# A weights-ring buffer for the window branch's key/value tiles, sets of four for two kinds of scores, and modulation products that wait for their last load

## The chip, the cores and the metric

One NeuronCore of one Trainium2 chip runs the whole kernel. The metric is the device time of one execution in microseconds (us); lower is better. The change is judged by the median of timed runs of the kernel before and after.

## The reference

One decoder layer for a prompt of 512 tokens and for 8 sample sequences of one token each, in float32. The layer's input is modulated by a vector that comes from a product with `w_ada`; one projection feeds a state-space branch (S5) and an attention branch with compressed, selected and window keys; then an output projection and an MLP follow.

```python
def hybrid_layer(x, c, ssm_s0, attend, lp):
    mod = jnp.dot(jax.nn.silu(c), lp['w_ada']) + lp['b_ada']        # 1024 -> 6144, for 1 + 8 rows
    sh1, sc1, gt1, sh2, sc2, gt2 = jnp.split(mod, 6, axis=-1)
    h = modulate(x, lp['norm_attn'], sh1, sc1)                      # rmsnorm(x) * (1 + sc1) + sh1
    proj = jnp.dot(h, lp['w_in'])
    u, q, k_c, v_c, k_s, v_s, k_w, v_w, g = jnp.split(proj, offsets, axis=-1)
    ...
    o_ssm, s_last = ssm_mixer(u, ssm_s0, lp)
    o_attn, win_state = attend(q, gates, kv_cmp, kv_slc, kv_win)
    mix = jnp.concatenate([rmsnorm(o_ssm, ...), rmsnorm(o_attn, ...)], axis=-1)
    x = x + gt1[:, None, :] * jnp.dot(mix, lp['w_out'])
    h2 = modulate(x, lp['norm_mlp'], sh2, sc2)
    x = x + gt2[:, None, :] * jnp.dot(jnp.square(jax.nn.relu(jnp.dot(h2, lp['w_up']))), lp['w_down'])
    return x, kv_cmp, kv_slc, win_state, s_last

def nsa_block(q, gates, ..., k_cmp, v_cmp, k_blk, v_blk, k_band, v_band, ...):
    p_cmp = masked_softmax(jnp.einsum('bgrqd,bngd->bgrqn', q, k_cmp), ...)
    ...                                          # the 16 best blocks are chosen from p_cmp
    p_slc = masked_softmax(jnp.einsum('bgrqd,bgqkjd->bgrqkj', q, k_sel), ...)
    p_win = masked_softmax(jnp.einsum('bgrqd,bkgd->bgrqk', q, k_band), ...)
```

The new keys and values (`kv_cmp`, `kv_slc`, `kv_win`) are outputs too.

## The kernel before, in words

**Who sets the order.** The kernel is written as straight code in Tile, and the framework is built with a scheduler that places every instruction on its engine's queue by a time that it models for it. Each queue then runs strictly in that order. So a dependence that the code adds changes the order of many instructions, not only of the one that waits. Loads go out on SyncE's queue (SP), most stores of the projections on ScalarE's (ACT), gathers on GpSimd's (POOL).

**Modulation (`ada`, lines 334 to 356).** The 6144 outputs are computed in 12 chunks of 512 columns, `ada0` to `ada11`. A chunk loads 1024x512 weights, in four loads of 512 KB or two of 1 MB (line 344, tile `wada`), and issues 8 products (line 348, tile `pada`): the stationary operand `cT[:, k]` has 32 columns, and product `k` writes rows `k % 4 * 32` of the result, so products 0 to 3 use four different groups of 32 columns of TensorE's array, and 4 to 7 add to them. ACT copies the result out (line 350), four transposes turn it (line 353, `padt`), and VectorE (DVE) sums it into `mod` (line 355). Chunks 0 to 3 are shift and scale of the first modulation; `hf`, `hH` and `hL` (lines 213 to 215), the modulated input as a high and a low part, need them, and the projection `pj` (line 619) needs `hH` and `hL`. The products `ph` (line 401), which compress the cached keys and values, and their transposes `pxc` (line 382) fill the first stage beside it.

**Key/value projections (`kv_proj`, from line 635).** Called for the compressed (0), selected (1) and window (2) branch. For each of four blocks of 128 tokens, ACT copies the result `pkv` into a tile `kvt` (line 672 or 688), sends it out by DMA (lines 673, 691, 692), and two transposes `pkt` (line 695) read it. `kvt` comes from a pool with two buffers. The large weights (`wkv`, `wq`, `wglu`, the halves of `wada`, `wo`, `wup`, `wdn`) come from a ring of three buffers, `rawt(name)`, each 128x2048 floats; a new tile waits until its buffer's last reader is done. `wq` (line 917) holds the queries' weights, which ACT and DVE split into `wH` and `wL` (lines 66, 67) for the query projection, again `pj`. `yc` (line 903) are small loads of the state-space branch's result, `rwin` (line 1165) the window rows of the sample sequences.

**Scores.** `compressed_scores` (from line 1170) computes `psc`: two sets of four products 128x32 by 128x512, one per head, each into its own 32 rows; the head's queries are ready after DVE's subtraction into `QS` (line 929). `sample_keys` (from line 1028) is called four times: for each set of four sequences, 16 transposes `pkT` (line 1038) and four copies `ktS` (lines 1041 and 1043, ACT for even, DVE for odd) give the keys, and four products `pS` (line 1047) the scores, again each into its own 32 rows. Six such sets exist. Between them lies the prompt's attention (`pst`, lines 1232 to 1234; `ptp`, line 1261; `po`, line 1268).

**State-space steps.** `u` is stored to scratch memory (`uscr`, lines 632 and 633) and loaded in another layout (`U<-uscr`, line 735), and `pvs` (line 805) reads it.

The dense end (`pwo`, `pup`, `pdn`, line 1427) takes the rest of the time.

Of the kernel before, what the change touches and what calls it, by code (L numbers as in the profile page):

```python
# [17 lines left out]
P = 128  # L18
# [19 lines left out]
def body(tc, i, o, dbg=None):  # L38
# [22 lines left out]
        return bank["tile"].tile([P, 512], F32, tag=tag, name=name, bufs=bank["tags"][tag])  # L61

    banks("pA", pj=2, ss=2, tr=2, ad=1, po=1)

    def split(h, l, src):
        nc.scalar.copy(h, src)  # L66
# [266 lines left out]
    def ada(s, tag, parts=2):  # L333

        ps = pst(tag, "pada")
        kp = KT // parts
        rs = []
        for n in range(parts):
            if parts == 2:
                r = rawt("wada")  # L340
            else:
                r = wp.tile([P, 1120], F32, tag=("wH", "wL")[n % 2], name="wada", bufs=2)[:, 0:1024]
            r = r.rearrange("p (k c) -> p k c", k=kp)
            nc.sync.dma_start(r, i["w_ada"][0, n * kp * P : (n + 1) * kp * P, s * 512 : (s + 1) * 512].rearrange("(k p) c -> p k c", p=P))
            rs.append(r)

        for k in range(KT):
            nc.tensor.matmul(ps[k % 4 * 32 : k % 4 * 32 + 32], cT[:, k], rs[k // kp][:, k % kp], start=(k < 4), stop=(k >= 4))
        mrow = wp.tile([P, 520], F32, tag="mrow", name="mrow")[:, 0:512]
        nc.scalar.copy(mrow, ps)  # L350
        pt = pst(tag, "padt")
        for m in range(4):
            nc.tensor.transpose(pt[:, m * P : (m + 1) * P], mrow[:, m * P : (m + 1) * P], ident)
        ms = mod[:, 4 * s : 4 * s + 4]
        nc.vector.tensor_reduce(ms, pt.rearrange("p (m q c) -> p m c q", m=4, q=4)[:, :, 0:9], AX.X, ALU.add)
        nc.vector.tensor_tensor(ms, ms, v_ada[:, 4 * s : 4 * s + 4].unsqueeze(2).to_broadcast([P, 4, 9]), ALU.add)
# [276 lines left out]
            nc.sync.dma_start(uscr[q * P : (q + 1) * P, T:NT], uT[q][:, T:NT])  # L633

    onames = ("cmp", "slc", "win")

    def kv_proj(c):
        c0 = 1024 + 256 * c
# [7 lines left out]
        for kk in range(2):  # L646
            kr = slice(4 * kk, 4 * kk + 4)
            h, l = whl(4, nw)
            split(h[:, :, 0:256], l[:, :, 0:256], r[:, kr])
            if c == 2:  # L650
                split(h[:, :, 256:280], l[:, :, 256:280], rg[:, kr])
            ws.append((h, l))
        for t in range(5):
            tok = slice(t * P, t * P + (P if t < 4 else NB))
            mp = P if t < 4 else NB
# [10 lines left out]
                else:  # L666
                    nc.scalar.dma_start(o["new_win_sample"][:, T - 1], kvs[:, 512:768])
            else:
                kvt = p1.tile([P, 256], F32, tag="kvt", name="kvt", bufs=2)
                out = o["new_%s_prompt" % onames[c]][tok]  # L670
                if c == 0:
                    nc.scalar.copy(kvt, ps[:, 0:256])
# [242 lines left out]
    for s in range(2):  # L915
        r = rawt("wq").rearrange("p (k c) -> p k c", k=KT)
        nc.sync.dma_start(r, i["w_in"][0, :, 512 + s * 256 : 512 + (s + 1) * 256].rearrange("(k p) c -> p k c", p=P))
        for m in range(2):
            wh, wl = wsplit(r[:, :, m * P : (m + 1) * P])
            h0 = 2 * (2 * s + m)  # L920
            for hf, ps in proj_half(wh, wl):
                ql = wp.tile([P, 520], F32, tag="mrow", name="ql")[0:64].rearrange("p (a b) -> p a b", a=2)
                w = min(HB, T - hf * HB)
                for hh in range(2):
                    pq_ = ps[hh * 64 : hh * 64 + 64]
                    qc = (h0 + hh, slice(hf * HB, hf * HB + w))
                    nc.scalar.activation(ql[:, hh], pq_, AF.Copy, scale=HD**-0.5)
                    nc.scalar.activation(QS[0:64, *qc], pq_[:, 0:w], AF.Copy, scale=HD**-0.5)
                    nc.vector.tensor_tensor(QS[64:128, *qc], ql[:, hh, 0:w], QS[0:64, *qc], ALU.subtract)
            nc.gpsimd.tensor_copy(qs[:, h0 : h0 + 2], ql[:, :, HB - NB : HB])  # L930
        state_space_outputs((2 + s,))
    dump("gates", gates)
# [96 lines left out]
    def sample_keys(br, grp, tiles, nj, gate):  # L1029
# [3 lines left out]
        for h in range(nj // 4):  # L1033
            kts = []
            for b4 in range(4):
                px = pst(("ad", "ss")[b4 % 2], "pkT")
                for j4 in range(4):
                    nc.tensor.transpose(px[:, j4 * P : (j4 + 1) * P], tiles[b4][:, 4 * h + j4, 0:P], ident)  # L1038
                kt = sb.tile([P, 512], F32, tag="ktS", name="ktS", bufs=4)
                if b4 % 2:  # L1040
                    nc.vector.tensor_copy(kt, px)
                else:
                    nc.scalar.copy(kt, px)
                kts.append(kt)
            S = pst("ss", "pS")
            for b4 in range(4):
                nc.tensor.matmul(S[b4 * 32 : b4 * 32 + 32], q4[:, 4 * grp + b4], kts[b4], start=True, stop=True)  # L1047
            if br == 0:
                nc.vector.tensor_tensor(t[:, h * 512 : (h + 1) * 512].rearrange("p (j k c) -> p j k c", j=4, c=8),
                                        S.rearrange("p (j k c) -> p j k c", j=4, c=8),  # L1050
# [119 lines left out]
    def compressed_scores():  # L1170
        for g in range(2):
            ps = pst("ss", "psc")
            for hh in range(4):
                nc.tensor.matmul(ps[hh * 32 : hh * 32 + 32], Kcp[:, g], QS[:, 4 * g + hh].bitcast(F32), start=True, stop=True)  # L1174
            nc.scalar.copy(etc[:, g], ps)

    held = {}
# [72 lines left out]
    def values(br, h0, pes, po):  # L1250

        kb = 2 * br + h0 // 4
        for part in (((0, 0),), ((1, 0), (3, 3 * P)), ((2, 0),)):
# [12 lines left out]
            for kt, c0 in part:  # L1266
                for hh, PT in enumerate(PTs):
                    mm = nc.tensor.matmul(po[hh * 64 : hh * 64 + 64, kt * P : T], Vx[:, kt, kb], PT[:, c0 : c0 + T - kt * P],  # L1268
                                          start=(br == 0 and kt == 0), stop=False)
                    if hh == 0:  # L1270

                        tc.add_manual_dep(mm.ins, turned_.ins.name, mybir.DependencyInfo(mybir.DependencyClass.Sync, mybir.DependencyReason.DATA))

    glu_w = []
    mixs = {}
# [354 lines left out]
```

## Time and profile before

| | |
|---|---|
| median of 3 runs | 900.21 us (898.96 to 900.66) |
| profiled execution, device time | 896.71 us |
| its span in the trace | 895.0 us |
| TensorE busy (PE) | 845.8 us, 94% |
| VectorE (DVE) | 519.8 us, 58% |
| ScalarE (ACT) | 389.9 us, 44% |
| dense end, 520 to 895 us | PE busy 366.98 of 375 us |

The span is the time between the first and the last instruction of the trace; the device time has 1.71 us around it. The profiled execution is 3.5 us below the median of the timed runs. A float32 product stands in the trace as two records, so "x4" of such a product is two matmuls. In a timeline row, the number behind the start is the length of a group of like instructions in a row; "[1.67 <-DMA ...]" is the time that the engine stood idle before it and what ended that.

### The profile page before, as it was taken

Reading aid. Unit: us, or ns where it says so; the run is one execution under the profiler, and the core shown is the slowest. Engines: PE = TensorE matmul, PEld = TensorE weight load, DVE = VectorE, ACT = ScalarE, POOL = GpSimd, SP = SyncE. Lnnn points to the kernel's source line nnn. Section 1 sums busy time; section 2 is a strip of 40 time slices with the busy share of each in tenths; the row PEclk is TensorE's granted clock in tenths of the full one; section 3 lists DMA queues with packets and bytes.
Section 4 is the critical chain, followed back from the end, with each engine's and each line's share of the span. In section 5 each row is a group of like instructions: output and inputs, shape, how many; then the busy total and the mean of one; then the engine's idle time right before and its main releaser. Section 6 shows DMA issues by size and latency. Waiting matters only on the chain.

```text
span 895.0 us, 16400 instructions
## 1 busy us (share of the span) xinstructions
PE 845.8 (94%) x6527; PEld 751.8 (84%) x6527; DVE 519.8 (58%) x1365; ACT 389.9 (44%) x883; POOL 64.0 (7%) x147
## 2 busy tenths in 40 slices
PE   2799998999998999998989999999999999999996
PEld 1557997888987766756679989999999999999996
DVE  5876666785766466668667874442333444434533
ACT  1555317453435466556655554442111344433322
POOL 6001201000152100000000000000000000000000
PEclk9999998999999999999989999999999999999998
DMA  8957577473773441203266553333333333232302
GB/s 290 319 195 247 181 157 193 138 247 116 203 244 92 165 166 64 77 2 142 73 210 198 180 190 94 94 96 94 95 95 95 94 95 92 82 86 75 92 1 96
DMA packets 111836, 122.36 MB, mean 137 GB/s; under 512 B 24500, under 2 KB 91880, under 8 KB 109584
## 3 DMA queue, kind: packets, MB, share of 16 engines
q1 hardware_dynamic: 101968, 88.66, 32.8%
q0 software_dynamic: 5488, 29.99, 9.6%
q10 hardware_dynamic: 4304, 2.66, 1.1%
q8 instruction: 51, 0.84, 0.4%
q14 instruction: 25, 0.20, 0.1%
HBM read 112.47 MB, written 13.03 MB: 140 GB/s over the span
## 4 chain that ended last, share of the span: by engine, by line
PE 66%; DVE 2%; ACT 1%; issue 0%; ACTq 0%; DVEq 0%
PE pup L1427 21%; PE pdn L1427 21%; PE pwo L1427 5%; PE pj L619 3%; PE po L1268 2%; PE ptp L1261 2%; PE pg L1289 2%; PE pS L1047 2%; PE pst L1232 1%; PE pkT L1038 1%; PE pst L1233 1%; PE psc L1174 1%; PE pstat L879 1%; PE poS L1136 0%; PE po L1349 0%; PE pst L1234 0%
## 5 line engine op out<-in xcount | busy, mean ns | idle before, releaser
L1427 PE MATMUL pdn<-hidH,wL 128*128 128x256 f32 (+1 forms) x480 | 136.0, 283 | 0.0
L1427 PE MATMUL pdn<-hidL,wH 128*128 128x256 f32 (+1 forms) x480 | 135.8, 283 | 0.0
L1427 PE MATMUL pup<-h2L,wH 128*128 128x256 f32 (+1 forms) x480 | 135.5, 283 | 0.0
L1427 PE MATMUL pdn<-hidH,wH 128*128 128x256 f32 (+1 forms) x480 | 135.3, 282 | 0.0
L1427 PE MATMUL pup<-h2H,wL 128*128 128x256 f32 (+1 forms) x480 | 135.0, 282 | 0.0
L1427 PE MATMUL pup<-h2H,wH 128*128 128x256 f32 (+1 forms) x480 | 134.5, 283 | 0.0
L1427 PEld LDWEIGHTS pup<-h2L,wH 128*128 128x128 f32 x480 | 90.4, 188 | 0.8 <-DVE rs L105 0.8
L1427 PEld LDWEIGHTS pup<-h2H,wH 128*128 128x128 f32 x480 | 89.8, 188 | 0.8 <-ACT h2H L66 0.8
L1427 PEld LDWEIGHTS pdn<-hidH,wL 128*128 128x128 f32 x480 | 90.4, 188 | 0.0
L1427 PEld LDWEIGHTS pdn<-hidL,wH 128*128 128x128 f32 x480 | 90.2, 188 | 0.1
L1427 PEld LDWEIGHTS pup<-h2H,wL 128*128 128x128 f32 x480 | 90.3, 188 | 0.0
L1427 PEld LDWEIGHTS pdn<-hidH,wH 128*128 128x128 f32 x480 | 90.3, 188 | 0.0
L66 ACT CAST wH<-wdn 128x1024 fp32r<-128x1024 f32 x30 | 31.5, 1049 | 114.2 <-PE pdn L1427 104.3
L67 DVE TENSOR_TENSOR wL<-wup,wH 128x1024 fp32r<-128x1024 f32 x30 | 36.7, 1225 | 57.9 <-ACT wH L66 57.9
L67 DVE TENSOR_TENSOR wL<-wdn,wH 128x1024 fp32r<-128x1024 f32 x30 | 36.8, 1225 | 54.3 <-ACT wH L66 54.3
L401 PE MATMUL ph<-xc,w 128*128 128x256 f32 (+2 forms) x320 | 62.9, 346 | 0.7 <-DVE xc L391 0.7
L401 PEld LDWEIGHTS ph<-xc,w 128*128 128x128 f32 x320 | 50.8, 194 | 11.0 <-issue 5.4
L66 ACT CAST wH<-wup 128x1024 fp32r<-128x1024 f32 x30 | 31.5, 1050 | 47.3 <-PE pup L1427 37.5
L1507 ACT ACTIVATE rl<-pup 128x256 f32<-128x256 f32 (+1 forms) x64 | 24.5, 385 | 45.5 <-PE pup L1427 45.4
L389 ACT COPY xc<-pxc 64x256 f32<-64x256 f32 x96 | 32.1, 366 | 22.5 <-DVE xc L391 18.8
L1508 DVE TENSOR_TENSOR rl<-rl 128x256 f32<-128x256 f32 (+1 forms) x64 | 27.2, 426 | 22.9 <-ACT rl L1507 22.9
L1436 DVE SCALAR_TENSOR_TENSOR xT<-pdn,mod,xT 128x256 f32<-128x256 f32 x32 | 15.2, 478 | 41.7 <-PE pdn L1427 41.6
(569 smaller groups left out, 2038.8 us busy)
## 6 DMA issues: line engine op xcount, KB each, us to landing
wada<-w_ada SPq DMA_DIRECT2D x20, 1024.0 KB, 5.1
wup<-w_up SPq DMA_DIRECT2D x16, 1024.0 KB, 5.4
wdn<-w_down SPq DMA_DIRECT2D x16, 1024.0 KB, 5.7
wo<-w_out SPq DMA_DIRECT2D x8, 1024.0 KB, 5.5
wada<-w_ada SPq DMA_DIRECT2D x8, 512.0 KB, 16.0
rwin<-state_win SPq DMA_DIRECT2D x4, 1024.0 KB
new_win_sample<-state_win POOLq DMA_DIRECT2D x2, 2044.0 KB, 8.6
wkv<-w_in SPq DMA_DIRECT2D x3, 1024.0 KB, 8.1
```

The lines of the kernel that those rows point to most:

```text
L66: nc.scalar.copy(h, src)
L67: nc.vector.tensor_tensor(l, src, h, ALU.subtract)
L389: nc.scalar.copy(dst[:, :, :, hf], srcv[:, :, :, hf])
L401: nc.tensor.matmul(phv[:, lo:hi, 0:w], w1[n][:, r_], xc[n][:, lo:hi, r_ % 8, off : off + w], start=(r_ == 0), stop=(r_ == 15))
L619: nc.tensor.matmul(ps[:, 0:HB], w[:, k], x[:, k, hc], start=(k == 0 and n == 0), stop=(k == KT - 1 and n == 2))
L1047: nc.tensor.matmul(S[b4 * 32 : b4 * 32 + 32], q4[:, 4 * grp + b4], kts[b4], start=True, stop=True)
L1261: nc.tensor.transpose(pt_[:, c : c + P], at(qt, kt * P, P), ident)
L1268: mm = nc.tensor.matmul(po[hh * 64 : hh * 64 + 64, kt * P : T], Vx[:, kt, kb], PT[:, c0 : c0 + T - kt * P], start=(br == 0 and kt == 0), s ...
L1289: nc.tensor.matmul(ps[:, 0:HB], r[:, k, c], zf[k][:, hc], start=(k == 0), stop=(k == 3))
L1427: nc.tensor.matmul(ps[:, 0 : b - a], w, x[:, a:b], start=first and n == 0, stop=last and n == 2)
L1507: nc.scalar.activation(rl, ps[:, 0 : b - a], AF.Relu)
L1508: nc.vector.tensor_tensor(rl, rl, rl, ALU.mult)
```

## The change

Four edits and a helper. `not_before(mm, last)` adds a dependence: matmul `mm` is not started before `last` is done. The existing dependence in the prompt's value products now goes through the helper and stays as it was.

- In `ada`, the first of the 8 products waits for the chunk's last load, where before each product waited for its own part of the weights.
- In `kv_proj(2)`, the four tiles `kvt` are four quarters of one buffer of the weights' ring, where before they came from the pool of two.
- In `sample_keys`, the first of the four products `pS` waits for the copies of the third and the fourth key tile.
- In `compressed_scores`, the first of the four products `psc` waits for the last head's subtraction into `QS`.

```diff
+    def not_before(mm, last):
+
+        tc.add_manual_dep(mm.ins, last.ins.name, mybir.DependencyInfo(mybir.DependencyClass.Sync, mybir.DependencyReason.DATA))
...
-            nc.sync.dma_start(r, i["w_ada"][0, n * kp * P : (n + 1) * kp * P, s * 512 : (s + 1) * 512].rearrange("(k p) c -> p k c", p=P))
+            landed = nc.sync.dma_start(r, i["w_ada"][0, n * kp * P : (n + 1) * kp * P, s * 512 : (s + 1) * 512].rearrange("(k p) c -> p k c", p=P))
             rs.append(r)
 
         for k in range(KT):
-            nc.tensor.matmul(ps[k % 4 * 32 : k % 4 * 32 + 32], cT[:, k], rs[k // kp][:, k % kp], start=(k < 4), stop=(k >= 4))
+            mm = nc.tensor.matmul(ps[k % 4 * 32 : k % 4 * 32 + 32], cT[:, k], rs[k // kp][:, k % kp], start=(k < 4), stop=(k >= 4))
+            if k == 0:
+                not_before(mm, landed)
...
+    qlast = {}
...
+        kvr = rawt("kvt") if c == 2 else None
...
-                kvt = p1.tile([P, 256], F32, tag="kvt", name="kvt", bufs=2)
+                kvt = kvr[:, t * 256 : (t + 1) * 256] if c == 2 else p1.tile([P, 256], F32, tag="kvt", name="kvt", bufs=2)
...
-                    nc.vector.tensor_tensor(QS[64:128, *qc], ql[:, hh, 0:w], QS[0:64, *qc], ALU.subtract)
+                    qlast[h0 + hh] = nc.vector.tensor_tensor(QS[64:128, *qc], ql[:, hh, 0:w], QS[0:64, *qc], ALU.subtract)
...
-                if b4 % 2:
-                    nc.vector.tensor_copy(kt, px)
-                else:
-                    nc.scalar.copy(kt, px)
-                kts.append(kt)
+                kts.append((kt, (nc.scalar.copy, nc.vector.tensor_copy)[b4 % 2](kt, px)))
             S = pst("ss", "pS")
             for b4 in range(4):
-                nc.tensor.matmul(S[b4 * 32 : b4 * 32 + 32], q4[:, 4 * grp + b4], kts[b4], start=True, stop=True)
+                mm = nc.tensor.matmul(S[b4 * 32 : b4 * 32 + 32], q4[:, 4 * grp + b4], kts[b4][0], start=True, stop=True)
+                if b4 == 0:
+
+                    not_before(mm, kts[2][1])
+                    not_before(mm, kts[3][1])
...
-                nc.tensor.matmul(ps[hh * 32 : hh * 32 + 32], Kcp[:, g], QS[:, 4 * g + hh].bitcast(F32), start=True, stop=True)
+                mm = nc.tensor.matmul(ps[hh * 32 : hh * 32 + 32], Kcp[:, g], QS[:, 4 * g + hh].bitcast(F32), start=True, stop=True)
+                if hh == 0:
+                    not_before(mm, qlast[4 * g + 3])
```

How the scheduler's order moves is shown at three places. In these rows, "x8" counts instructions, and the changed kernel's line numbers are a few higher (348 becomes 352, 353 becomes 359, 401 becomes 407).

First, TensorE in the first stage, where chunk 0's products stand among the compression's products. Before (its first two products stand a few rows earlier):

```order
L348 MATMUL pada<-wada,cT 32x512 x2
L401 MATMUL ph<-xc,w_160 128x128 x3
L348 MATMUL pada<-wada,cT 32x512 x2
L401 MATMUL ph<-xc,w_160 128x128 x6
L449 MATMUL pss<-ones,xsq 8x1 x8
L401 MATMUL ph<-xc,w_160 128x128 x3
L401 MATMUL ph<-xc,w_161 128x130 x3
L348 MATMUL pada<-wada,cT 32x512 x2
L401 MATMUL ph<-xc,w_161 128x130 x13
```

Changed:

```order
L407 MATMUL ph<-xc,w_160 128x130 x4
L449 MATMUL pxs<-ident,xsr 128x64
L407 MATMUL ph<-xc,w_160 128x128 x16
L407 MATMUL ph<-xc,w_161 128x130
L455 MATMUL pss<-ones,xsq 8x1 x8
L407 MATMUL ph<-xc,w_161 128x130 x14
L352 MATMUL pada<-wada,cT 32x512 x8
L407 MATMUL ph<-xc,w_161 128x130
```

The four runs of two are one run of eight, behind 35 products `ph`. Of all chunks: before, the runs are 2+2+2+2 (chunk 0), 1+2+1+4 (chunk 1), 4+4 (chunks 2 to 6), 5+3 (7), 2+6 (8) and 8 (9 to 11); changed, 5+3 (chunk 4), 1+4+3 (chunk 8) and 8 for each other. `psc` goes from six runs (2, 2, 1, 1, 1, 1) to two of four, and `pS` from 13 runs to six of four.

Second, TensorE ahead of the first projection `pj`, where chunk 3, the last that the modulated input needs, is turned (`padt`). `px` are the transposes of the input itself. Before:

```order
L348 MATMUL pada<-wada,cT 32x512 x4
L592 MATMUL px<-ident,xr 128x128 x8
L401 MATMUL ph<-xc,w_160 128x2x128 x2
L353 MATMUL padt<-ident,mrow 128x128 x4
L592 MATMUL px<-ident,xr 128x128 x8
L401 MATMUL ph<-xc,w_161 128x2x128 x10
```

Changed:

```order
L352 MATMUL pada<-wada,cT 32x512 x8
L598 MATMUL px<-ident,xr 128x128 x8
L407 MATMUL ph<-xc,w_161 128x2x128 x10
L359 MATMUL padt<-ident,mrow 128x128 x4
L598 MATMUL px<-ident,xr 128x128 x8
L416 MATMUL pk<-hg,w2k 64x128 x2
L407 MATMUL ph<-xc,w_161 128x2x128 x6
```

Chunk 3's turn now stands behind ten products `ph` that followed it, and chunk 4's first half no longer stands ahead of `pj`.

Third, SP's queue around the loads of the queries' weights. Before:

```order
L835 DMA yscr<-ys 128x320
L917 DMA wq<-w_in 128x8x256 x2
L787 DMA Tz<-mscr 128x8x64
L785 DMA mscr<-M_2487 128x64
L903 DMA yc<-yscr 16x8x80 x4
L787 DMA Tz<-mscr 128x8x64
L903 DMA yc<-yscr 16x8x80 x2
L835 DMA yscr<-ys 128x320
L903 DMA yc<-yscr 16x8x80 x5
L835 DMA yscr<-ys 128x320
L903 DMA yc<-yscr 16x8x80
L1279 DMA wglu<-ssm_w_glu 128x4x512
```

Changed:

```order
L912 DMA yc<-yscr 16x8x80 x7
L796 DMA Tz<-mscr 128x8x64
L912 DMA yc<-yscr 16x8x80
L844 DMA yscr<-ys 128x320
L912 DMA yc<-yscr 16x8x80 x4
L844 DMA yscr<-ys 128x320
L926 DMA wq<-w_in 128x8x256 x2
L912 DMA yc<-yscr 16x8x80 x4
L1174 DMA rwin<-state_win 128x2x1024 x3
L1289 DMA wglu<-ssm_w_glu 128x4x512
```

The new buffer takes the ring's place that `wq`'s first half had, so both halves move one place on, to the buffers of the last two `wkv`, and in the queue behind the last store of `yscr`; `wglu` moves behind `rwin`.

## Rows read from the trace of the kernel before

**Rows 1.** The page's head and its busy shares.

```profile
span 895.0 us, 16400 instructions
...
PE 845.8 (94%) x6527; PEld 751.8 (84%) x6527; DVE 519.8 (58%) x1365; ACT 389.9 (44%) x883; POOL 64.0 (7%) x147
```

**Rows 2.** Windows: length; busy PE, PEld, DVE, ACT, POOL; clock; DMA share; GB/s.

```profile
80.00:100.00 20.00, 19.34 (x136) 15.82 (x134) 18.64 (x44) 11.93 (x23) 6.49 (x14) 1.00 0.80 272
...
140.00:145.00 5.00, 5.00 (x25) 4.80 (x24) 2.89 (x8) 3.53 (x12) 0.40 (x1) 0.51 0.14 47
...
270.00:275.00 5.00, 2.38 (x14) 1.48 (x13) 2.73 (x9) 3.88 (x10) 1.41 (x3) 0.96 0.48 108
275.00:280.00 5.00, 5.00 (x32) 5.00 (x32) 3.12 (x6) 1.72 (x5) 1.04 (x1) 0.70 0.28 45
...
400.00:420.00 20.00, 17.13 (x173) 13.02 (x172) 16.11 (x45) 13.90 (x41) 1.93 (x2) 1.00 0.42 158
```

**Rows 3.** Waits of TensorE, whole span: total us, times, longest.

```profile
PE pada L348 <- DMA wada<-w_ada: 4.3, 3, 2.0
```

**Rows 4.** Timeline of TensorE: runs of two, four and eight modulation products.

```profile
36.30 1.05 PE L348 MATMUL pada<-wada,cT 128*32 128x512 f32 x4 [1.67 <-DMA wada<-w_ada]
37.28 0.94 PE L401 MATMUL ph<-xc,w 128*128 128x128 f32 x6
...
89.57 1.06 PE L348 MATMUL pada<-wada,cT 128*32 128x512 f32 x8 [0.66 <-DMA wada<-w_ada]
90.56 1.09 PE L592 MATMUL px<-ident,xr 128*128 128x128 f32 x8
...
225.80 1.92 PE L348 MATMUL pada<-wada,cT 128*32 128x512 f32 x16
```

**Rows 5.** Timeline of TensorE: a run of two `psc` and one of one.

```profile
287.33 1.05 PE L1174 MATMUL psc<-QS,Kcp 128*32 128x512 f32 x4
288.31 0.39 PE L619 MATMUL pj<-hH,wH 128*128 128x260 f32 x1
...
302.92 1.04 PE L1174 MATMUL psc<-QS,Kcp 128*32 128x512 f32 x2
303.89 0.29 PE L1011 MATMUL pgs<-gates,e8h 8*64 8x24 f32 x2
```

**Rows 6.** Timeline of TensorE: a run of one `pS`.

```profile
386.83 1.05 PE L1047 MATMUL pS<-ktS,q 128*32 128x512 f32 x2
387.81 0.66 PE L1038 MATMUL pkT<-ident,rslc 128*128 128x128 f32 x4
```

**Rows 7.** Timelines of ACT and TensorE around the window branch's `kvt`.

```profile
266.68 0.37 ACT L688 COPY kvt<-pkv 128x256 f32<-128x256 f32 x1 [2.87 <-DMA new_win_prompt<-kvt]
...
270.67 0.37 ACT L688 COPY kvt<-pkv 128x256 f32<-128x256 f32 x1 [3.35 <-DMA new_win_prompt<-kvt]
...
272.03 1.04 ACT L66 CAST wH<-wq 128x1024 fp32r<-128x1024 f32 x1 [0.46 <-PE pkv L660]
...
271.10 0.44 PE L695 MATMUL pkt<-ident,kvt 128*128 128x128 f32 x2 [0.74 <-ACT kvt L688]
...
273.12 0.39 PE L619 MATMUL pj<-hH,wH 128*128 128x260 f32 x1 [1.33 <-ACT wH L66]
```

**Rows 8.** Timelines of DVE and TensorE: from the last chunk's sum to the projection.

```profile
79.72 0.31 DVE L355 TENSOR_REDUCE mod<-padt 128x36 f32<-128x144 f32 x1
...
94.64 0.74 DVE L215 SCALAR_TENSOR_TENSOR hL<-hf,mod,hH 128x512 fp32r<-128x512 f32 x1
...
80.39 4.48 PE L401 MATMUL ph<-xc,w 128*128 128x256 f32 x20
```

**Rows 9.** Timelines: TensorE's first `pvs`; SP's loads of `wq` and last store of `yscr`.

```profile
137.91 1.82 PE L805 MATMUL pvs<-U,Bb 128*128 128x72 f32 x8 [3.46 <-DMA new_cmp_prompt<-kvt]
...
226.93 1.76 SPq L917 DMA_DIRECT2D wq<-w_in  x2
...
253.41 0.43 SPq L835 DMA_DIRECT2D yscr<-ys  x1
```

More of the change, by code (lines that the diff above doesn't have):

```diff
@@ L1270, in values @@
                     if hh == 0:
-                        tc.add_manual_dep(mm.ins, turned_.ins.name, mybir.DependencyInfo(mybir.DependencyClass.Sync, mybir.DependencyReason.DATA))
+                        not_before(mm, turned_)
     glu_w = []
```

## The prediction

> **What bounds the kernel now.** I read the page's head first: TensorE is busy 845.8 of 895.0 us, DVE 58%, ACT 44% [rows 1]. So time goes down only where TensorE's own work gets shorter or one of its few waits goes. Then the waits of TensorE: those that the change can touch are 4.3 us on modulation weights [rows 3], 3.46 us at the first `pvs` [rows 9], and a knot around the window branch's `kvt` [rows 7]. Then the windows, for the granted clock and for stretches where another engine is as full as TensorE: 80 to 100 us, where DVE works 18.64 of 20, and 400 to 420 us, where DVE works 16.11, ACT 13.90 and TensorE 17.13 [rows 2]. Last, the timeline at each small product with 32 stationary columns. The reader is to see there that such a run costs by sets, not by products: from the start of a run to the start of the next work it takes 0.98 us for two products, 0.97 for one [rows 5], 0.98 for one `pS` [rows 6], 0.98 for two `pada` and 0.99 for four [rows 4]. Eight, which are two sets of four, took 1.92 [rows 4]. A set split into two runs pays its 0.98 twice. This is what three of the four edits are about.
>
> **`psc`.** Six runs become two, by the order in the section on the change: 6 x 0.98 = 5.9 us become 2 x 0.99 = 2.0. Saved: 3.9 us of TensorE. The work around them is plain `pj` and transposes that follow directly, so I take it whole. The added wait is for a subtraction that the last product of the set needed anyway. Bounds 3.0 to 3.9 us, the lower end if one gate stops TensorE for about a set's length. **-3.9.**
>
> **`pS`.** 13 runs become six: 7 x 0.98 = 6.9 us of TensorE. Here not all of it need reach the end: DVE and ACT make the keys' copies and the softmax beside it, and in 400 to 420 us TensorE idles 2.87 us already [rows 2]. Each gate also puts the set behind the last two copies, with `psn`, `pst` and `ptp` queued behind it. Bounds: 2 us (only the sets away from that window pay) to 6.9 us. I take seven tenths, since TensorE is near full in most of the stretch. **-4.8.** The Trainium skill, "TensorEngine Tiling (Array Packing)", section "PSUM Bottleneck", says that tiling speeds up TensorE but not the copies out of PSUM, which may become the limit. By that, this term would be near its lower end; the window 400 to 420 us leans that way, with TensorE at 17.13 of 20.
>
> **Modulation products.** A chunk of eight costs 1.9 us as one run. Chunk 0 in four runs costs 3.9, so 2.0 goes; chunk 1, also four runs, the same 2.0. Two runs of four cost 1.98, so chunks 2, 3, 5 and 6 give 0.1 each. Chunk 7 (5+3, about 1.9 + 1.0) gives 1.0. Chunk 4 is now 5+3 and loses 0.9. Chunk 8 (2+6, then 1+4+3) stays about even at 2.9. Sum: 4.5 us. To this come the three waits on weights, 4.3 us, two of them in chunk 0, where 35 products `ph` now stand ahead instead [rows 3, 4].
>
> But the first stage ends on another chain. Chunk 3's turn (`padt`) feeds DVE, and from DVE's sum at 79.72 to the last `hL` at 95.4 lie 15.7 us in which DVE is almost full [rows 2, 8]. Up to that turn TensorE gains at most 2.0 + 2.0 + 0.2 and the two waits in chunk 0, 3.6 us (4.3 less the 0.66 of the third): 7.8. Yet the turn moves behind ten products `ph`, which took 4.48 us [rows 8]. That leaves 3.3, and chunk 2's loads now go out only when all of chunk 0's products have freed their buffers. I take 2.0 at the projection, and 0.7 for the rest (the third wait, and chunks 4 to 8 net). Bounds: 0.3 (the turn comes no earlier) to 8.8 (all of 4.5 and 4.3, DVE no limit). Nearest to the DVE rows is the low half. **-2.7.**
>
> **`kvt` from the ring.** ACT's third and fourth copy wait 2.87 and 3.35 us until the first two tiles' stores have landed, and the casts of `wq` stand behind them on ACT; TensorE then waits 0.74 at `pkt` and 1.33 at `pj` [rows 7]. In 270 to 275 us TensorE is idle 5.00 - 2.38 = 2.6 us, and in the next 5 us it runs at 0.70 of full clock, which loses 1.5 us [rows 2]: 4.1 us in all. With four tiles this wait cannot be. What comes next there is `wq` itself: it moves from 226.93 us to behind the last `yscr` store at 253.41 [rows 9], and an activation of the state-space branch now stands between a copy and its store on ACT. From 253.8 to the cast at 272.03 are 18 us. At the rate of 80 to 100 us, 272 GB/s at a share of 0.80, a free queue carries its 2.1 MB in an estimated 6.2 us. `wglu` moves back too, but its products come only in the attention stage. I take 3.5 of 4.1; bounds 0 to 4.1. **-3.5.**
>
> **The first `pvs`.** It waits 3.46 us, and the clock then falls to 0.51 for 140 to 145 us, 2.5 us lost [rows 2, 9]. The scheduler now puts eight transposes ahead of it, before four of them and four products. That hides a little more; the loads of `U` that it really awaits keep their place. Bounds: 2.7 us worse (1 MB of weights on the same queue, at that rate an estimated 3.1 us, arrives beside them) to 3.5 better. **-0.5.**
>
> **Sum.** 3.9 + 4.8 + 2.7 + 3.5 + 0.5 = 15.4 us. The profiled execution took 896.71, so 881.3; the median of the timed runs lies 3.5 above it, so the forecast is **884.8 us**, with 879 to 890 as its own range.
>
> **Rivals.**
>
> *DVE and ACT hold both stages.* The turn comes no earlier, so modulation gives 0.3, and of `pS` 1.5 is left: 3.9 + 1.5 + 0.3 + 3.5 + 0.5 = 9.7, about 890.5 us. For it: DVE at 18.64 of 20, and the turn's place in the order. Against: in most of the attention stage TensorE is the fuller one. Chance 0.22.
>
> *`wq` comes late: slower.* Its loads now leave 27 us later, behind `yc` and `yscr`, in a stretch where DMA also carries the window rows. If TensorE runs dry for n us at the query projection, it pays n, and then again about as much at half clock: after 3.46 us of waiting it ran at 0.51, the lower of the two levels (1.2 GHz) [rows 2, 9]. The other terms give 11.9, so the kernel is slower from n = 6; at n = 8 it is 16 - 11.9 = 4.1 over, 904.3 us. Against: the 18 us above. Chance 0.09. The Trainium skill, "TensorE: Matmul & The Clock Gate", section "HAM oscillation — how this bites in real kernels", describes the same: a TensorE that runs dry on DMA falls to the cold clock and begins the next work there. By that, the wait's price doubles as computed; the trace agrees at 140 to 145 us, with 0.51.
>
> *Everything pays.* The first stage gains its 8.8 and `pvs` its 3.5: about 20 to 25 us, some 877 or less. Chance 0.06.
>
> *The change does not do what it says:* a run of four on the chip costs more than a run of one, or the gates hold TensorE as long as the sets save. About 900.2. Rows 4 and 5 speak against the first. Chance 0.03.
>
> **How the numbers follow.** The forecast has the remaining 0.60. A measurement of this kernel can tell about 0.2%, 1.8 us. Faster by more: 0.60 + 0.22 + 0.06 less a small tail = 0.87; the same 0.04; slower 0.09. The range of 877 to 896 takes in the forecast and the first rival with the lower ends of `kvt` and `pvs`; it leaves out the slow rival, no change and most of the case in which everything pays, 0.18 together.
>
> **What would show it.** Right: `psc` in two rows of x8 and `pS` in six, each about 1 us; no wait of ACT's `kvt` on the window branch's stores; full clock from 270 to 280 us; the waits on `wada` under 2 us in total. The first `pj`, right behind the transposes at 90.56 us [rows 4], should begin 2 us earlier, and the end of the attention stage some 15 us earlier. Wrong: TensorE waiting for `wH` of `wq` by more than 2 us; a gate (`pada` on `wada`, `pS` on `ktS`) with a wait over 1 us; the first `pj` no earlier than before, or as much as 6 us earlier, which would be the first-stage term mis-sized.

## The result and the profile after

The changed kernel took 887.29 us in the median of 4 runs (886.10 to 889.05), the kernel before 899.59 in 4 runs beside it (898.59 to 900.66). The ratio is 0.9865, with a 95% interval of 0.984 to 0.989: 12.3 us less, where 15.4 were forecast. The profiled execution of the changed kernel took 888.46 us, 1.2 above its median; that of before lies 2.9 below its own. So the two traces differ by only 8.2 us of span. Stages below are compared between these two traces, one execution each; the other 4.1 us of the 12.3 cannot be placed in a stage.

The page's head and busy shares of the changed kernel:

```profile
span 886.8 us, 16421 instructions
...
PE 837.3 (94%) x6527; PEld 756.2 (85%) x6527; DVE 521.1 (59%) x1365; ACT 389.1 (44%) x883; POOL 64.2 (7%) x147
```

TensorE works 8.5 us less than in [rows 1], about what the span lost, and is as full as before. A run of products below is a group of them that follow each other directly on TensorE. The two sets of `psc`, in TensorE's timeline of the changed kernel (in its second column, a group's length):

```profile
293.25 1.07 PE L1183 MATMUL psc<-QS,Kcp 128*32 128x512 f32 x8
294.25 0.39 PE L625 MATMUL pj<-hH,wH 128*128 128x260 f32 x1
...
303.31 1.06 PE L1183 MATMUL psc<-QS,Kcp 128*32 128x512 f32 x8
304.31 0.66 PE L1047 MATMUL pkT<-ident,rwin 128*128 128x128 f32 x4
```

Four products now cost 1.00 us from start to start, what one or two cost in [rows 5]. The waits of TensorE over the span that answer to the forecast:

```profile
PE pj L625 <- DVE hL L219: 2.8, 3, 1.0
...
PE pvs L814 <- DMA new_cmp_sample<-kvs: 2.5, 1, 2.5
...
PE pxc L388 <- ACT xc L395: 2.2, 4, 1.0
...
PE pada L352 <- DMA wada<-w_ada: 1.1, 2, 0.6
PE psn L1065 <- ACT ktS L1049: 1.1, 2, 0.7
...
PE pS L1052 <- DVE ktS L1049: 0.4, 1, 0.4
```

The gates themselves hold TensorE little: 1.1 us at the modulation's weights (4.3 in [rows 3]) and 0.4 at the keys' copies. New are 1.1 us at `psn`, a product behind `pS` that needs the same copies, 2.8 us on `hL` and 2.2 on `xc`; the kernel before had no such wait at `psn` or on `hL`, and 0.4 on that `xc`. The windows of the changed kernel (columns as in [rows 2]; a clock of 0.50 is the lower of TensorE's two levels, 1.2 GHz, and a value between is the mean of a stretch that has both):

```profile
80.00:100.00 20.00, 16.81 (x101) 15.35 (x100) 19.07 (x42) 9.78 (x19) 4.07 (x9) 0.83 0.39 138
90.00:95.00 5.00, 5.00 (x25) 5.00 (x25) 4.80 (x13) 0.72 (x1) 0.00 (x0) 0.50 0.01 3
...
160.00:180.00 20.00, 17.83 (x109) 15.89 (x107) 12.21 (x29) 11.11 (x32) 0.86 (x4) 0.94 0.37 108
180.00:185.00 5.00, 5.00 (x25) 3.60 (x29) 3.87 (x14) 3.75 (x12) 0.13 (x1) 0.50 0.03 7
180.00:200.00 20.00, 20.00 (x111) 14.55 (x111) 12.58 (x34) 7.43 (x21) 1.12 (x5) 0.81 0.56 181
...
270.00:275.00 5.00, 5.00 (x42) 4.08 (x40) 3.09 (x11) 1.96 (x5) 2.26 (x5) 1.00 0.52 148
275.00:280.00 5.00, 5.00 (x42) 4.74 (x39) 4.94 (x10) 3.03 (x8) 1.11 (x1) 1.00 1.04 411
400.00:420.00 20.00, 17.44 (x111) 13.23 (x109) 15.77 (x43) 13.24 (x40) 0.00 (x0) 0.91 0.32 128
```

The knot at 270 to 280 us is gone: TensorE full, clock at 1.00, where [rows 2] had 2.38 of 5 us and 0.70. In its place the clock is down in three stretches where it was not: 0.83 from 80 to 100 us, 0.94 and 0.81 from 160 to 200, and 0.91 from 400 to 420. The kernel before in the second of them:

```profile
160.00:180.00 20.00, 19.16 (x128) 15.72 (x126) 13.57 (x36) 10.63 (x30) 0.93 (x5) 1.00 0.40 127
180.00:200.00 20.00, 20.00 (x120) 16.29 (x120) 17.32 (x47) 10.59 (x30) 2.09 (x8) 1.00 0.79 257
```

By stages, from the first and last starts of `pkv`, `pj` and `pwo` in each trace:

| stage | before | after | difference |
|---|---|---|---|
| start to the first key/value product | 116.5 | 115.9 | -0.6 |
| to the last product of the query projection | 185.7 | 184.1 | -1.6 |
| attention, to the first `pwo` | 140.2 | 134.2 | -6.0 |
| dense end | 452.6 | 452.6 | 0.0 |

The forecast had put 4.0 us on the second row for `kvt` and `pvs`, and two of the four saved runs of `psc` lie in it, another 2.0; only 1.6 came. The first `pj` starts at 82.97 us, 8.4 earlier than before (91.41), and yet the first key/value product only 0.6 earlier.

### The profile page after: what moved, and what is told of

It reads as the page before. It is cut to its first block, busy times and chain, and to the rows that moved or that the text cites. A ratio compares the mean times of both kernels' runs of the same rounds, so it can differ in the third digit from the quotient of the medians.

```text
span 886.8 us, 16421 instructions
## 1 busy us (share of the span) xinstructions
PE 837.3 (94%) x6527; PEld 756.2 (85%) x6527; DVE 521.1 (59%) x1365; ACT 389.1 (44%) x883; POOL 64.2 (7%) x147
## 4 chain that ended last, share of the span: by engine, by line
PE 85%; DVE 8%; ACT 3%; DMA 3%; issue 1%; SPq 1%; DVEq 0%; ACTq 0%
PE pdn L1437 21%; PE pup L1437 21%; PE pj L625 5%; PE pwo L1437 5%; PE pkv L669 5%; PE ph L407 4%; PE pada L352 2%; PE po L1279 2%; PE ptp L1272 2%; PE pg L1299 2%; PE pys L841 2%; ACT xc L395 1%; DVE xc L397 1%; PE pkT L1047 1%; PE pst L1243 1%; DMA rslc<-cache_slc,pidx 1%
## 5 line engine op out<-in xcount | busy, mean ns | idle before, releaser
L1437 PE MATMUL pup<-h2L,wH 128*128 128x256 f32 (+1 forms) x480 | 135.6, 283 | 0.0
L1437 PE MATMUL pup<-h2H,wH 128*128 128x256 f32 (+1 forms) x480 | 134.5, 283 | 0.0
L70 ACT CAST wH<-wdn 128x1024 fp32r<-128x1024 f32 x30 | 31.4, 1048 | 114.2 <-PE pdn L1437 104.4
L1253 ACT ACTIVATE pe<-pst,mxa 128x512 f32<-128x512 f32 (+1 forms) x64 | 33.6, 535 | 15.7 <-DVE mxa L1249 13.4
```

Source lines behind the costliest of these rows:

```text
L1253: nc.scalar.activation(at(qt, 0, nk), d, AF.Exp, bias=mx[:, qt : qt + 1], accum_out=dn[:, qt : qt + 1])
L1437: nc.tensor.matmul(ps[:, 0 : b - a], w, x[:, a:b], start=first and n == 0, stop=last and n == 2)
```

## The experiments

The first four take one edit each and put it on the kernel before; their diffs show the edit's core, against that kernel. Every ratio is to the kernel before, timed beside the experiment, with a 95% interval; a difference in us is one of medians, where nothing else is said. Stage times come from one trace of each kernel.

### The gate of the compressed scores alone

```diff
+                if hh == 0:
+                    not_before(mm, qlast[4 * g + 3])
```

> The kernel before with the gate of the compressed scores alone. Forecast's term: two runs of four in place of six runs, 3.9 us less, about 895.7 us, and TensorE's waits elsewhere unchanged. Rival (the reordering around it gives the gain back): within 1.5 us of the kernel before, about 899.6.

Measured: 902.85 us, ratio 1.0038 (1.0019 to 1.0057). Slower, by 3.1 us, and neither expectation held. The local gain is there: the second stage shrank from 185.7 to 183.5 us. The attention stage grew from 140.2 to 146.5. I added up TensorE's time there by tile, from each start to the next in the timeline:

| attention stage, us | before | `psc` alone | `pS` alone | modulation alone | after |
|---|---|---|---|---|---|
| `psc` | 2.9 | 1.0 | 2.9 | 2.9 | 1.0 |
| `pS` | 13.5 | 15.4 | 6.0 | 16.4 | 6.0 |
| `poS` | 7.9 | 8.7 | 8.8 | 8.5 | 8.0 |
| idle | 5.3 | 8.5 | 6.1 | 6.1 | 7.4 |
| runs of `pS` | 13 | 15 | 6 | 16 | 6 |
| runs of `poS` | 8 | 12 | 12 | 10 | 9 |
| whole stage | 140.2 | 146.5 | 135.6 | 147.7 | 134.2 |

With `psc` gathered, the scheduler laid the attention out anew. It split `pS` into 15 runs and `poS`, the sample's value products, into 12, and TensorE waited 3.2 us more. One of the sets of `pS` in this run, now in three runs (TensorE's timeline):

```profile
388.10 1.05 PE L1049 MATMUL pS<-ktS,q 128*32 128x512 f32 x4
389.08 0.55 PE L1265 MATMUL ptp<-ident,pe 128*128 128x128 f32 x3
389.56 1.05 PE L1049 MATMUL pS<-ktS,q 128*32 128x512 f32 x2
390.54 0.66 PE L1044 MATMUL pkT<-ident,rslc 128*128 128x128 f32 x4
391.13 1.04 PE L1049 MATMUL pS<-ktS,q 128*32 128x512 f32 x2
392.10 0.66 PE L1044 MATMUL pkT<-ident,rslc 128*128 128x128 f32 x4
```

Three times 0.98 for four products. The edit's own gain was real, and the order that it caused elsewhere cost more: the rows of the table account for 4.0 of the 6.3 us that the stage lost, and the other 2.3 lie on other tiles.

### The gate of the sample scores alone

```diff
+                if b4 == 0:
+                    not_before(mm, kts[2][1])
+                    not_before(mm, kts[3][1])
```

> The kernel before with the gate of the sample scores alone. Forecast's term: 4.8 us less, about 894.8. What the two traces suggest: the stretch from the query projection's end to the last sample set became 7.5 us shorter, so about 892. Rival (DVE and ACT hold the stage): 1.5 us less, about 898.1.

Measured: 890.80 us, ratio 0.9902 (0.9877 to 0.9928), 9.0 us less, nearest to what the two traces suggested. `pS` went from 13.5 to 6.0 us of TensorE. The attention stage is 4.6 us shorter, and the stretch behind it, to the end, 449.5 against 452.6 us. Of those last 3.1 us, 1.6 are clock and not the edit's sets: from 440 to 480 us it stood at 0.97 and 0.86 in the kernel before and at 0.91 and 1.00 here. The stage's idle time rose by only 0.8 us, so DVE and ACT do not hold this stage.

### The modulation products' gate alone

```diff
+            if k == 0:
+                not_before(mm, landed)
```

> The kernel before with the modulation products' gate alone. Forecast's term: 2.7 us less, about 896.9. What the two traces suggest: the projection starts about 8 us earlier but waits for DVE's hL, so the first key/value product comes under 1 us earlier, and the middle stage, to the prompt's compression, loses some 6 us to the new order and to TensorE's lower clock: 3 to 5 us slower than before, about 903.

Measured: 907.22 us, ratio 1.0073 (1.0049 to 1.0098), 7.5 us slower. The direction of what the traces suggested, and more than it. The first stage gained 1.4 us (115.1), the second lost 4.3 (190.0), and the attention stage lost 7.5 (147.7): without their own gate the sample scores were split into 16 runs, 2.9 us more of TensorE in the table above, and the clock fell in a place where it had not, to 0.83 from 320 to 340 us, which loses 20 x 0.17 = 3.4 us.

### The key/value tiles in the ring alone

```diff
+        kvr = rawt("kvt") if c == 2 else None
...
-                kvt = p1.tile([P, 256], F32, tag="kvt", name="kvt", bufs=2)
+                kvt = kvr[:, t * 256 : (t + 1) * 256] if c == 2 else p1.tile([P, 256], F32, tag="kvt", name="kvt", bufs=2)
```

> The kernel before with the window branch's key/value tiles in the weights' ring alone. Forecast's term: 3.5 us less, about 896.1, with TensorE full and at full clock from 260 to 280 us. Rival (the loads of the queries' weights, 30 us later on the queue, bring a wait of their own): no faster than before, about 899.6, and TensorE waiting for the cast of those weights.

Measured: 893.25 us, ratio 0.9935 (0.9911 to 0.9959), 6.5 us less; by the spans, 890.6 against 895.0, 4.4. The second stage went from 185.7 to 181.3 us and carries all of it. In the window from 260 to 280 us TensorE works 18.52 us at a clock of 1.00, where the kernel before, first row, had 17.04 at 0.91:

```profile
260.00:280.00 20.00, 17.04 (x118) 15.05 (x117) 10.76 (x25) 7.50 (x22) 5.26 (x10) 0.91 0.70 230
...
260.00:280.00 20.00, 18.52 (x146) 16.96 (x145) 14.44 (x30) 10.25 (x29) 5.03 (x10) 1.00 0.95 325
```

The late load of the queries' weights does not hold this kernel: ACT's idle time before their cast, 0.81 us at 269.84 us, is ended by TensorE. In this run a wait of 1.3 us for their cast stays at the projection, as long as in [rows 7]; in the changed kernel there is none.

The four single results add up to -4.9 us; together the edits gave 12.3. They are not independent: each one changes the order of the stages behind it.

### Without the modulation gate

From here on the diffs are against the changed kernel, where nothing else is said.

```diff
-            if k == 0:
-                not_before(mm, landed)
```

> The changed kernel without the modulation products' gate; the other three edits stay. Theory: that gate gains nothing at the first key/value product (0.6 us in the two traces) and costs some 6 us between there and the prompt's compression, so without it about 881 us, with the compression starting near 213 us as before the change. Rival, the forecast's term (the gate is worth 2.7 us): about 890.

Measured: 884.43 us, ratio 0.9825 (0.9803 to 0.9846), against 0.9865 with the gate. The gate costs 0.0040 of 899.6, 3.6 us (2.9 between the medians); the two intervals touch, so the size is loose. The forecast's sign for it was wrong. The theory's 881 was 3.4 us too low. The second stage is 178.9 us, 5.2 less than in the changed kernel.

### The gate on the first four chunks, and on the others

```diff
-            if k == 0:
+            if k == 0 and s < 4:
                 not_before(mm, landed)
```

> The changed kernel with the gate on chunks 0 to 3 only. Theory: the first projection starts some 8 us earlier and then waits for DVE; the first key/value product stays where it was within 1 us, so about 881, as without any gate. Rival (the early start, with its waits and its lower clock, is what the later stages lose by): about 887.

Measured: 883.52 us, ratio 0.9823 (0.9803 to 0.9844), as without any gate. The first key/value product stands at 116.3 us (116.5 before; 118.6 in the run without any gate, which lost 1.8 us at a clock of 0.91 from 40 to 60 us). In the time, the first stage's gathered runs show neither a gain nor a cost.

```diff
-            if k == 0:
+            if k == 0 and s >= 4:
                 not_before(mm, landed)
```

> The changed kernel with the gate on chunks 4 to 11 only. Theory: the middle stage's new order costs its 6 us, with TensorE waiting for xc near 175 us and a stretch at the lower clock behind it, so about 887, as the changed kernel. Rival (the first stage is the cause): about 881, with the compression starting near 213 us.

Measured: 890.62 us, ratio 0.9888 (0.9869 to 0.9907). The second stage is 185.0 us. So the loss comes from the chunks behind the fourth, as the theory said. The time is higher than it said, with an interval that overlaps the changed kernel's. The profiled execution, at 896.47 us, is the slowest of the six; it lost 5.2 us to the clock (0.89 and 0.85 from 20 to 60 us), ahead of every gated chunk.

### Both score gates

> The kernel before with the gates of compressed and sample scores together. Theory (what counts in the attention stage is how many runs the small column products form, 27 before, 29 with the compressed gate alone, 24 with the sample gate alone, 17 here, at about 1 us each): about 10 us less, about 889.5. Rival (the two single results, +3.1 and -9.0, add up): about 894.

The edit is the first two diffs together. Measured: 889.90 us, ratio 0.9880 (0.9863 to 0.9898), 10.5 us less than the kernel before. The singles would add up to 6. With both gates the attention stage is 134.5 us long. The gate of `pS` takes away what the gate of `psc` alone had suffered from. Beside the gate of `pS` (0.9902 alone), that of `psc` is worth 0.0022, 2.0 us, and the two intervals overlap. The count of runs gave the right size here, but it is not the whole: in the run with `psc` alone, 3.2 us of the 6.3 that the stage lost were waits.

### The gate on every chunk but chunk 6

The changed kernel between 174 and 184 us, TensorE's timeline. `pxc` are transposes whose results ACT copies to `xc`; `pada` is chunk 6:

```profile
174.54 0.66 PE L789 MATMUL pbb<-ident,BP 128*128 128x128 f32 x4 [0.55 <-ACT Vp L249]
175.85 0.66 PE L388 MATMUL pxc<-ident,rc 128*128 128x128 f32 x4 [0.65 <-ACT xc L395]
177.47 1.12 PE L388 MATMUL pxc<-ident,rc 128*128 128x128 f32 x4 [0.97 <-ACT xc L395]
178.38 1.82 PE L814 MATMUL pvs<-U,Bb 128*128 128x72 f32 x8
180.00 1.82 PE L788 MATMUL pm<-C,BP 128*128 128x16 f32 x8
...
183.53 3.64 PE L352 MATMUL pada<-wada,cT 128*32 128x512 f32 x16
```

TensorE waits three times for ACT's copies out of PSUM, then runs at half clock: `pada` takes 3.64 us, nearly twice the 1.92 of [rows 4]. The same three waits (0.55, 0.66, 0.97) and the same 3.64 stand in the run with the gate on the later chunks. The kernel before did chunk 6 as two runs of four between the groups of `pxc`, while ACT copied:

```profile
170.57 1.04 PE L382 MATMUL pxc<-ident,rc 128*128 128x128 f32 x8
171.53 1.07 PE L348 MATMUL pada<-wada,cT 128*32 128x512 f32 x8
...
177.82 0.60 PE L382 MATMUL pxc<-ident,rc 128*128 128x128 f32 x4
178.35 1.07 PE L348 MATMUL pada<-wada,cT 128*32 128x512 f32 x8
```

```diff
-            if k == 0:
+            if k == 0 and s != 6:
                 not_before(mm, landed)
```

> The changed kernel with the gate on every chunk but chunk 6. Theory: in the middle stage chunk 6's two halves were what TensorE did while ACT copied pxc out; as one run behind them they leave TensorE waiting for those copies, and the lower clock follows. Without chunk 6's gate the stretch from the first key/value product to the compression is 96 to 98 us (103.5 in the changed kernel), and the time about 882.5 us. Rival (another gated chunk, or the loads' order on SP's queue, is the cause): the stretch stays over 101 us, and the time about 887.

The same place in this run:

```profile
170.07 1.04 PE L388 MATMUL pxc<-ident,rc 128*128 128x128 f32 x8
171.04 1.06 PE L352 MATMUL pada<-wada,cT 128*32 128x512 f32 x8
...
176.23 0.66 PE L388 MATMUL pxc<-ident,rc 128*128 128x128 f32 x4 [0.56 <-ACT xc L395]
177.45 1.07 PE L352 MATMUL pada<-wada,cT 128*32 128x512 f32 x8 [0.56 <-DMA wada<-w_ada]
178.45 0.66 PE L388 MATMUL pxc<-ident,rc 128*128 128x128 f32 x4
178.94 1.01 PE L814 MATMUL pvs<-U,Bb 128*128 128x72 f32 x8
```

Measured: 881.82 us, ratio 0.9814 (0.9791 to 0.9837). From the first key/value product to the compression it takes 95.8 us (103.5 in the changed kernel, 96.3 before), and the clock stays at 1.00 from 160 to 200 us. Over all traces, this stretch is 100.6 to 104.4 us in the three with chunk 6 gathered (the modulation gate alone, the changed kernel, the gate on the later chunks) and 95.8 to 97.2 in the ten others. So chunk 6, gathered, is what the modulation gate loses by in this stretch. (Chunk 8 moved too: 4+4 here, where the changed kernel has 1+4+3, one run more, for which about 1 us of the 7.7 would account. No run gathers chunk 6 alone.) The kernel beats the changed one beyond both intervals. From the runs with no gate and with the gate on the first four, it cannot be told apart.

### Chunk 3's turn ahead of the compression's products

In the changed kernel DVE's sum of chunk 3 starts at 77.70 us (79.72 in [rows 8]), and TensorE, then ahead, waits for DVE piece by piece (TensorE's timeline, changed kernel):

```profile
77.06 0.60 PE L359 MATMUL padt<-ident,mrow 128*128 128x128 f32 x4
...
82.97 0.39 PE L625 MATMUL pj<-hH,wH 128*128 128x260 f32 x1 [0.40 <-DVE gx L329]
...
85.94 0.39 PE L625 MATMUL pj<-hL,wH 128*128 128x260 f32 x1 [0.90 <-DVE hL L219]
...
87.60 0.39 PE L625 MATMUL pj<-hL,wH 128*128 128x260 f32 x1 [0.99 <-DVE hL L219]
...
89.12 0.59 PE L625 MATMUL pj<-hL,wH 128*128 128x260 f32 x1 [0.90 <-DVE hL L219]
```

The projection starts at 82.97 us, and the first key/value product behind it still comes at 115.9. The next kernel has the gate on chunks 0 to 3 and moves the turn:

```diff
+                    if bp == 1 and n == 1 and r_ == 0:
+                        not_before(mm, padt[3])
```

Here `mm` is the first product `ph` of the second half of the second pair of sequences, and `padt[3]` chunk 3's last transpose.

> The kernel with the gate on chunks 0 to 3 only, and one dependence more: the second half of the compression's products of the second pair of sequences waits for chunk 3's turn, so the turn stands ahead of nine of them. Theory (DVE's chain from the turn to the last hL sets when the projection ends its first part): the turn comes some 4 us earlier and the first key/value product 2 to 4 us earlier than 116.3, about 880.5 us if the later stages keep their order. Rival (something else, as the weights' loads or TensorE's own work, bounds the first stage): the first key/value product within 1 us of 116.3, about 883.5.

Measured: 882.20 us, ratio 0.9821 (0.9799 to 0.9842), the same as without the dependence. DVE's sum came at 74.15 us, 3.5 earlier, and TensorE had no wait on `hL`; but the first key/value product came at 115.6, as the rival said. What stands in this kernel's first stage is another wait (TensorE, 60 to 300 us):

```profile
PE pada L354 <- DMA wada<-w_ada: 3.8, 2, 2.4
```

These are chunk 4's two halves, which this kernel does ahead of and inside the projection; the run with the gate on chunks 0 to 3 alone had 4.5 us of the same wait. The last run has both: chunk 3's turn early, and the gate on every chunk but chunk 6, which moves chunk 4 to the projection's end.

> The changed kernel with the gate on every chunk but chunk 6 and with chunk 3's turn ahead of nine of the compression's products. Theory: with the turn early DVE's hL is in time, and with chunk 4 gated its loads no longer stand in TensorE's way at the projection, so both waits of the two runs before (2.6 us on hL, 3.8 us on weights) are gone; the first key/value product comes 3 to 5 us earlier than 116.2, about 878 us. Rival (TensorE's own work bounds the projection): the first key/value product within 1.5 us of 116.2, about 881.

Measured: 883.39 us, ratio 0.9815 (0.9795 to 0.9836). The theory held for its stage: the first key/value product came at 112.1 us, 4.1 earlier than without the early turn. Of that, 3.4 are clock: from 80 to 100 us it stands at 1.00, where the run without the early turn has 0.83. The end did not follow; the theory's 878 was 5 us too low. Against the run without the early turn, the last `po` of the attention stage came 1.0 us later and the span ended 2.1 us later. Between 420 and 460 us stand new waits and a lower clock, first in this run, then in the one without the early turn:

```profile
420.00:440.00 20.00, 17.59 (x174) 13.31 (x172) 10.32 (x31) 11.29 (x25) 0.96 (x1) 0.91 0.73 251
440.00:460.00 20.00, 17.70 (x113) 15.92 (x112) 14.69 (x41) 12.40 (x25) 0.00 (x0) 0.83 0.20 66
```

```profile
420.00:440.00 20.00, 18.98 (x191) 13.52 (x189) 11.43 (x33) 13.38 (x30) 0.96 (x1) 1.00 0.60 210
440.00:460.00 20.00, 17.86 (x124) 16.51 (x123) 15.43 (x43) 13.40 (x26) 0.00 (x0) 0.91 0.41 130
```

The clock alone costs 20 x 0.09 + 20 x 0.08 = 3.4 us there, and TensorE is idle 1.6 us more. Whether this comes from the scheduler's new order there or from an unlucky meeting of engines is open; no run held the attention's order fixed.

## Why the prediction was right, and where it was wrong

The time fell in the range, with the sign forecast, 2.5 us above the forecast. The sum was closer than its terms, and that is in part luck: without the modulation gate the other edits took 15.7 us (ratio 0.9825), where their terms with `pvs` come to 12.7, and the modulation term was 6.3 us off the other way.

Of the signs named ahead, `psc` in two rows, `pS` in six, no wait of ACT's `kvt` on the window branch's stores, the full clock from 270 to 280 us and 1.1 us on `wada` came as said. One sign of being wrong came too: the first `pj` starts 8.4 us earlier, past the 6 that the prediction named for a mis-sized first-stage term. And the attention stage ends 8.2 us earlier in the traces, not some 15.

**`psc`, -3.9: the size was right.** TensorE's time on it went from six runs to two of 1.00 us. But that this would reach the end whole was not borne out: alone the edit made the kernel 3.1 us slower, with other sets split and new waits, and beside the gate of `pS` it is worth 2.0 us, within the intervals. "The work around them ... I take it whole" was the weak sentence.

**`pS`, -4.8: right in kind; the size held between the two traces, not for the edit alone.** TensorE saved 7.5 us (6.9 forecast, because one of the 13 runs took 1.7). Between the two traces the stage's idle time rose by 2.1, so 5.4 were left, close to the seven tenths. The run with this edit alone gained more, 9.0 us: 4.6 in this stage, and a part behind it that the term does not speak of. The stage as a whole fell by 6.0: 5.4 and 1.9 of `psc`, less 1.3 on other tiles, for which the clock of 0.91 from 400 to 420 us (20 x 0.09 = 1.8 us) would account. DVE and ACT showed as those 2.1 us of waits and not as a bound. The Trainium skill, "TensorEngine Tiling (Array Packing)", section "PSUM Bottleneck", says that the copies out of PSUM may become the limit once tiling speeds up TensorE. The trace agrees in the direction, with those 2.1 us; the copies did not become the limit here.

**Modulation, -2.7: wrong sign; it cost about 3.6.** Of the first stage, the part on DVE was right: the turn moved from 79.72 to 77.70 us, the 2.0 that I took. The part on TensorE was not: the projection began 8.4 us earlier, but with DVE's chain only 2.0 earlier it then waited 2.8 us on `hL` and lost 3.4 us at a clock of 0.83, and 0.6 us were left at the first key/value product. That DVE's lateness would also cost clock is in no term. The last run above agrees with that chain by moving it: with the turn and chunk 4 out of the way, that stage is 4.1 us shorter. The step that failed is "0.7 for the rest (the third wait, and chunks 4 to 8 net)". I had counted chunk 6's two halves as 0.1 us to be gained. They were filler: they covered ACT's copies, and gathered they uncovered waits of 0.55, 0.65 and 0.97 us and a stretch at the lower clock. That they stood between groups of `pxc` could be read from the order.

**`kvt`, -3.5: right in kind, a little small.** The run with it alone gained 4.4 by the spans (6.5 by the timed runs); the window from 260 to 280 us accounts for 3.3 of that, 1.5 of idle time and 1.8 of clock. Beside both score gates the edit is worth 0.0055, 5.0 us (0.9880 against 0.9825). I had kept 0.6 back for a wait on `wq`. In the changed kernel that load left at 259.3 us and its cast began at 273.9, ACT's last idle time before it ended by TensorE and not by the load. The slow rival did not come true. It was not without ground: in the run with the gate on every chunk but chunk 6, ACT waited 2.17 us before that cast for a DMA (the profile names a load of `yc`; the cast itself reads only `wq`), and TensorE then 0.66 us.

**`pvs`, -0.5: not settled.** The wait fell from 3.46 to 2.5 us, and the clock from 140 to 145 us is 0.67 instead of 0.51. But the first `pvs` began at 138.4 instead of 137.91, and no run isolates this term.

Of the rivals, the one in which DVE holds the first stage came true there and not in the attention stage. What no rival had was that each edit re-lays the later stages. Single edits came out -4 to +10 us from their forecast terms, more than most of those terms; that the new order did all of it is argued and not shown, since no run held the order fixed.

## What to carry to other kernels

A run of small column-tiled products (here 128x32 by 128x512 in float32) costs by sets and not by products, 0.97 to 1.00 us for one, two or four. So a dependence that keeps a set together saves TensorE about 1 us for each run saved. What reaches the end can differ, and it holds only for the tiles that are gated, since the scheduler may split the others more than before (`pS` from 13 runs to 14, 15 and 16 when other edits came alone). Before gathering a set, look at what stands on both sides of its parts in the order: parts that lie between transposes and their copies are filler, and moving them uncovers the wait. With a scheduler in the loop, test edits both alone and left out: here one was worth -9.0 us, one +3.1 alone, and both together -10.5. Only the modulation gate was also left out of the four.

## What was not expected of the hardware

The granted clock fell without any long wait. In the kernel before, 0.51 in [rows 2] followed a single wait of 3.46 us. In the changed kernel it stood at half behind three waits of 0.55, 0.65 and 0.97 us between short transposes (0.50 from 180 to 185 us), and again behind three waits of 0.9 to 1.0 us on `hL` (0.50 from 90 to 95). The first of these stretches cost 20 x 0.06 + 20 x 0.19 = 5.0 us from 160 to 200 us, more than twice the waits ahead of it. With chunk 6's halves back in their places, two waits of 0.56 us were left there and the clock stayed at 1.00. At the first place the runs do not part the waits from the transposes that stand between them; at the second, products stand between the waits.

The Trainium skill, "TensorE: Matmul & The Clock Gate", section "A second HAM failure mode: psum-queue depth-cycling", describes such a case for bf16 products: TensorE, cycling through PSUM's banks, often idles briefly between groups of products, and the clock swings. The trace agrees with that at the first place, with 0.81 from 180 to 200 us, here with float32 and one fall; the second place, with its waits on a DVE result, is not that case.
